# Block 2 of a two-block kernel: POOL's work taken over by DVE, and the units of v put ahead of the convolved ones

## The chip, the cores and the metric

One core of a Trainium2 chip runs the kernel; the other cores do nothing. The metric is device microseconds of one execution, as the median of several. Three runs of the kernel before took 1039.68, 1042.36 and 1042.78 us. The engines are named as in the profile: PE multiplies matrices, DVE and POOL work on vectors, ACT evaluates functions and copies, SP issues the transfers.

## The reference

Two blocks work on 256 tokens of 1024 features in fp32. The first is a Mamba-like mixer followed by a mixture of 32 experts; the change doesn't touch it, except for its last additions to `h`. The second block, of which the change reorders the mixer's half, is

```python
h = rms_norm(x, norm1)
lru_x, lru_g, q, k, v, g, z = jnp.split(h @ w_in, SPLIT_IDX, axis=-1)
lru_x = causal_depthwise_conv_2(lru_x, conv_w, conv_b)
lru_o = rg_lru(lru_x, lru_wa, lru_ba, lru_wi, lru_bi, lru_lambda) * jax.nn.gelu(lru_g)
log_alpha = jax.nn.log_sigmoid(z @ gla_w_alpha + gla_b_alpha) / GATE_TAU
o = gla_chunk_causal(q * q_scale, k, v, log_alpha)
gla_o = rms_norm(o, gla_norm) * jax.nn.silu(g)
x = x + jnp.concatenate([lru_o, gla_o], axis=-1) @ w_out
```

`rg_lru` takes two sigmoids of small block-diagonal products of the convolved `lru_x`, and runs a linear recurrence over the tokens. `gla_chunk_causal` is a gated linear attention in four chunks of 64 tokens, whose decays come from `z`. A gated feed-forward network follows.

## The kernel before, in words

Every large product is done in three passes: a weight tile is split into a rounded part `hi` (ACT, L329) and the rest `lo` (L330), and PE adds hi by hi, hi by lo and lo by hi. One column tile of 128 outputs with 1024 inputs is a **unit**: a split, 24 products of 128x256 (L339 to L341), and an `after` that takes the result out of PSUM. A unit of v (`v_unit`) is two of the eight rows of inputs by all 512 columns, in 12 products of 128x512 (L1672 to L1674).

`run_units` writes the order out by hand, since the engines run their instructions in program order and wait by semaphores. In turn i it emits the work registered with `at_pre(i)`, the split of unit i+2, unit i's products, the `after` of unit i-1, and then the work registered with `at(i)`. There are four buffers each of `hi` and `lo`, so that the split of unit i+4 waits for unit i's products.

The units of block 2's mixer before are: 0 z; 1, 2 k; 3, 4 q; 5 to 8 lx (the convolved ones); 9 to 12 v; 13 to 16 lg; 17 to 20 g; 21 to 28 the output projection. The split of units 1 and 2 is done ahead, at block 1's end. The tuple `P2` names the units whose `lo` POOL computes instead of DVE: 4 to 12.

The row scales (the norm's reciprocal roots) come late, and unscaled products wait for them in PSUM. `sums2` takes the sums of squares on ACT, `scales2` (L1451 to L1455 and `rsqrt_of`) the roots on DVE, `across` (L286) writes them on a diagonal `dg`, and PE spreads them over the partitions (`rsp`, L290) ahead of unit `SCALE`, which is 5. From then on the waiting results of z, k and q are scaled into SBUF, and all later ones directly. z's own small product with `wal` (`zf`, L1604) follows one turn later; `zexp`, ten polynomial steps in pieces of `STEPS`, and `la` make the decays of it; two exponentials and `kq_decay` apply them to k and q.

A unit of lx is scaled into `rg` (L1516), weighted by ACT (L1519), convolved by three DVE steps (L1524, "rest"), multiplied with the block-diagonal weights `wab` by PE (`gate_mm`, L1537, two turns later and ahead of that turn's unit), passed through two sigmoids by ACT (L1542) and multiplied by POOL (`ix`, L1543). `lru_exp`, `lru_q` and `lru_u` prepare the recurrence. `k_turn`, `scores` and `update` are the attention's small products from turn 13 on; `attend` (L1741, L1744) uses the last state `st` ahead of unit 17.

Of the kernel before, what the change touches and what calls it, by code (L numbers as in the profile page):

```python
# [8 lines left out]
F32 = mybir.dt.float32  # L9
# [17 lines left out]
WARM3 = 10  # L27
WARM4 = 5
K1 = (0, 1)
SH1 = 1  # L30
STEPS = (4, 3)
GAINS = 15
P2 = (4, 5, 6, 7, 8, 9, 10, 11, 12)
KT = 13
LEAD = 5
WARM2 = 4
# [33 lines left out]
def kernel(ctx: ExitStack, tc: tile.TileContext, *aps, dbg=None, stage=9):  # L70
# [276 lines left out]
    def at(i, f, *args):  # L347
        due.setdefault(i, []).append((f, args))

    def later(n, f, *args):  # L350
        at(cur[0] + n, f, *args)
# [112 lines left out]
    wo2, wfi, wfo = A["w_out_2"][0], A["w_ffn_in_2"][0], A["w_ffn_out_2"][0]  # L464
    skip = [1, 1, 0, 0]
    R2 = {}
    loads2 = deque([("kq", 1024), ("lx", 0), ("v", 1536), ("lg", 512), ("g", 2048), (("wo", 0), 0), (("wo", 1), 0)])
    for c in range(11):
        loads2.append((("fi", c), 0))
        if c % 2 == 1:  # L470
# [3 lines left out]
    def load_next2():  # L474
        if loads2:
            nm, c0 = loads2.popleft()
            if nm[0] == "wo":
                R2[nm] = raw_rows(wo2, 4 * nm[1])
            elif nm[0] == "fo":
                R2[nm] = raw_rows(wfo, 4 * nm[1], min(4, NF - 4 * nm[1]))  # L480
            elif nm[0] == "fi":
                t = R2[nm] = raw_tile([128, 8, 2, 256])
                for i in range(2):
                    c0 = i * 128 * NF + nm[1] * 256
                    nc.sync.dma_start(t[:, :, i, :], wfi[:, c0:c0 + 256].rearrange("(k p) c -> p k c", p=128))
            elif nm == "kq":
                t = R2[nm] = raw_tile([128, 8, 512])
                for c in (256, 0):
                    nc.sync.dma_start(t[:, :, c:c + 256], wcols("w_in_2", c0 + c, 256))
            else:  # L490
                R2[nm] = raw_cols("w_in_2", c0)
# [98 lines left out]
    def col_unit(src, c0, after, m=128, tag="mm", lo_last=False):  # L590


        def sp():
            return hilo(src()[:, :, c0:c0 + m], (8, m))

        def mm(w):
            o = ps.tile([128, T], F32, name="mm", tag=tag, bufs={"mm": 3, "op": 2, "pp": 2}.get(tag, 1))
            if lo_last:
                for k in range(8):
                    P.matmul(o[:m], w[0][:, k, :], hnh[:, k, :], start=(k == 0), stop=False)  # L600
                    P.matmul(o[:m], w[0][:, k, :], hnl[:, k, :], start=False, stop=False)
                for k in range(8):
                    P.matmul(o[:m], w[1][:, k, :], hnh[:, k, :], start=False, stop=(k == 7))
                return o
            for k in range(8):
                mm3(o[:m], w[0][:, k, :], w[1][:, k, :], hnh[:, k, :], hnl[:, k, :], k == 0, k == 7)
            return o

        return sp, mm, after
# [279 lines left out]
    gains = []  # L889
# [237 lines left out]
    with ExitStack() as pp:  # L1127
# [240 lines left out]
        def last_rows(g):  # L1368
            for (a, n, ns), tag in zip(HALF, (("p2", 1), ("py0", 1), ("py1", 1), ("gp", 1))):
                combine(g, a, n, tag)  # L1370
                if not a:
                    G.tensor_tensor(X2["g"][:, a, ns], h[:, a, ns], gains[1][:, ns], op=ALU.mult)  # L1372
                if (a, n) == K1:
                    split2(1)
            sums2(h, "sh", 0)
            if not SH1:
                sums2(h, "sh", 1)

        def sums2(src, acc, a):
            for n in range(2):  # L1380
                S.activation(X2["x"], src[:, a, n * 512:(n + 1) * 512], AF.Square, accum_out=X2[acc][:, a, n:n + 1])
# [58 lines left out]
    with ExitStack() as pc:  # L1440
# [22 lines left out]
            dump("x2", h)  # L1463
            more_bufs()

        def gains2():
            for n in range(2):
                ns = slice(n * 512, (n + 1) * 512)
                V.tensor_tensor(X2["g"][:, 1, ns], h[:, 1, ns], gains[1][:, ns], op=ALU.mult)

        psm = ExitStack()
        ps = psm.enter_context(tc.tile_pool(name="psC", bufs=1, space=PSUM, reuse_waits="tile"))
# [1 line left out]
        def buf(name, tag=None, dt=F32):  # L1474
            return mw.tile([128, 4, T], dt, name=name, tag=tag or name)

        SCALE = 5


        wab = [mw.tile([128, 4, 128], F32, name=f"wab{i}", tag=f"wab{i}") for i in range(2)]  # L1480
# [59 lines left out]
        def gate_act(t, p):  # L1540
            for i, (dst, c) in enumerate(((rg, c_ba), (ix, c_bi))):
                S.activation(dst[:, t, :], p[:, i, :], AF.Sigmoid, bias=cols2[:, c + t:c + t + 1])  # L1542
            G.tensor_tensor(ix[:, t, :], ix[:, t, :], xf[:, t, :], op=ALU.mult)  # L1543


        def lru_exp(t):
            S.activation(al[:, t, :], rg[:, t, :], AF.Exp, scale=sp8[:, 4 + t:5 + t])
            S.activation(rg[:, t, :], rg[:, t, :], AF.Tanh, scale=sp8[:, t:t + 1])
            if t == 3:
                G.tensor_tensor(s2, al, al, op=ALU.mult)  # L1550

        def lru_q():
            V.scalar_tensor_tensor(s2, s2, 1.0, rg, op0=ALU.add, op1=ALU.mult)
# [53 lines left out]
        def zexp():  # L1607
            for j in range(2):
                V.tensor_scalar(zb[:, j, :], Z["p"][:, j, :], cols2[:, c_gb + j:c_gb + j + 1], None, op0=ALU.add)
            S.activation(zu, zb, AF.Abs)  # L1610
            S.activation(zu, zu, AF.Exp, scale=-1.0)
            S.activation(small.tile([128, 1], F32, name="one"), ones[:, 0:1], AF.Sigmoid)
            poly = log1p_steps(zu, za)
            def steps(n):
                for _ in range(n):
                    poly.pop(0)()
                if poly:
                    later(1, steps, STEPS[1])
                else:
                    later(1, la)  # L1620

            later(1, steps, STEPS[0])

        def la():
            V.scalar_tensor_tensor(zb, zb, 0.0, za, op0=ALU.min, op1=ALU.subtract)
            for j in range(2):
                V.tensor_tensor_scan(zu[:, j, :], cmask, zb[:, j, :], 0.0, op0=ALU.mult, op1=ALU.add)
            bv = zu.rearrange(c4, c=4)
            be = bv[:, :, :, 63:64]
            V.tensor_tensor(za.rearrange(c4, c=4), be.to_broadcast([128, 2, 4, 64]), bv, op=ALU.subtract)  # L1630
            later(2, lambda: [S.activation(za, za, AF.Exp, scale=1.0 / 16),
                              S.activation(eb.unsqueeze(3), be, AF.Exp, scale=1.0 / 16)])
            later(2, kq_decay)

        def kq_decay():
# [5 lines left out]
            return lambda o: V.tensor_tensor(kd[:, j, :], o, rsb, op=ALU.mult)  # L1641

        def after_q(j):
            def f(o):
                V.scalar_tensor_tensor(qs[:, j, :], o, 0.125, rsb, op0=ALU.mult, op1=ALU.mult)
                if j == 1:
                    load_next2()

            return f

        def k_turn():
            p = ps.tile([128, 2, 256], F32, name="tp", tag="tp")
# [51 lines left out]
        def scores(a):  # L1704
            sT[a] = mw.tile([128, 4, 128], F32, name="sT", tag=("zu", "za")[a])
            ts = slice(a * 128, (a + 1) * 128)
            for s in range(2):
                p = ps.tile([128, 2, 128], F32, name="sc", tag=("tq", "ss")[s])
                r = slice(s * 64, s * 64 + 64)
                for j in range(2):  # L1710
                    P.matmul(p[:, j, :], kd[r, j, ts], qs[r, j, ts], start=True, stop=True)
                later(0, lambda p=p, s=s: V.tensor_tensor(sT[a][:, s::2, :], p,
                                                          diag[:, None, :].to_broadcast([128, 2, 128]), op=ALU.mult))
# [122 lines left out]
        def src2(nm):  # L1836
            return lambda: R2[nm]

        def from_scale(f):
            return lambda o: at(SCALE, f, o)  # L1840

        units = [narrow_unit(lambda: wz2, from_scale(after_z), tag="ss")]
        units += [col_unit(src2("kq"), 256 + j * 128, from_scale(after_k(j))) for j in range(2)]
        units += [col_unit(src2("kq"), j * 128, from_scale(after_q(j)), tag=("mm", "op")[j])
                  for j in range(2)]
        units += [col_unit(src2("lx"), t * 128, after_lx(t), tag="mm" if t else "op") for t in range(4)]
        units += [v_unit(i) for i in range(4)]
        units += [col_unit(src2("lg"), t * 128, after_lg(t)) for t in range(4)]
        units += [col_unit(src2("g"), t * 128, after_g(t)) for t in range(4)]
        units += [row_unit2(i) for i in range(8)]  # L1850
# [13 lines left out]
            at_pre(23 + i, gla_scale, i)  # L1864
            at(23 + i, gla_split, i)
        for t in range(4):
            at(14 + t // 2, lru_exp, t)
        at(16, lru_q)
        at(17, lru_u)
        for t in range(4):  # L1870
# [1 line left out]
            at(19 + t // 2, lru_out, t)  # L1872
            at(20 + t // 2, lru_lo, t)
        at(18, lru_gelu)
        at(0, gains2)
        if SH1:
            at(1, sums2, h, "sh", 1)
        for a in range(2):
            at(2, sums2, X2["g"], "sg", a)
        at(2, scales2)  # L1880
        at_pre(SCALE, lambda: across_mm(dg, rsb, ps.tile([128, T], F32, name="rsp", tag="tq")))
        at(3, rows2_)
        at(1, masks)
        at(6, chunks)
        at(GAINS, lambda: gains.extend([gain_rows("norm2_2", nc.gpsimd), gain_rows("final_norm_2", nc.gpsimd)]))
        early3 = []
        for j in range(2):
            at(len(units) - 2 + j, lambda j=j: early3.append(hilo(R2["fi", 0][:, :, j, 0:128], (8, 128))))
        run_units(units, ready=early2, pool=lambda i: i in P2)
        psm.close()  # L1890
        mix.close()
        dump("x3", h)
# [145 lines left out]
```

## Time and profile before

| | |
|---|---|
| median of 3 runs | 1042.36 us (1039.68 to 1042.78) |
| the profiled execution | 1042.26 us, of which the span of its instructions is 1040.5 us |
| busy over the span | PE 884.6, PEld 625.4, DVE 433.0, ACT 318.5, POOL 146.9 us |
| PE on the chain that ended last | 27%, DVE 4%, DMA 1% |
| mean granted clock of PE | 0.907 |

The span falls into block 1's mixer (about the first 190 us), the experts, in which the transfers are busy nearly throughout (to about 715 us), block 2's mixer (715 to 845 us), and its feed-forward network. In the last 180 us PE is at work almost without a break. The change is in block 2's mixer, between 720 and 800 us of the span, and that is the stretch to read: for each idle time of PE, which engine ended it, and what that engine did meanwhile.

### The profile page before, as it was taken

How to read it: one execution, taken by the hardware profiler on the slowest of the kernel's cores; microseconds unless marked ns; L12 is line 12 of the kernel's file. 1: busy time of each engine (PE TensorE's matmuls, PEld its weight loads, DVE VectorE, ACT ScalarE, POOL GpSimd, SP SyncE). 2: the span in 40 equal slices, each digit the busy share in tenths (PEclk: the TensorE clock that was granted, in tenths of full speed). 3: DMA queues.
4: the chain of work that ended last, by engine and by line, in shares of the span. 5: the costliest groups of instructions: out<-in, count | busy, mean ns of one | idle time of the engine just before them, and what ended most of it. 6: DMA issues, size and time to landing. Idle time of an engine off the chain costs nothing. (4 is left out here: it accounts for less than half of the span.)

```text
span 1040.5 us, 13656 instructions
## 1 busy us (share of the span) xinstructions
PE 884.6 (85%) x5675; PEld 625.4 (60%) x5676; DVE 433.0 (42%) x756; ACT 318.5 (31%) x533; POOL 146.9 (14%) x127
## 2 busy tenths in 40 slices
PE   8999998999868695776768596679679999999997
PEld 8988887677414141412314151137668789999996
DVE  6897565653002010101001010104896677555554
ACT  6664454524001100000000000004456545444444
POOL 4232024001000000000000000001452222111112
PEclk9999998999878798788779788769889999999999
DMA  9594433357999999999999999996534435474401
GB/s 288 135 388 166 162 105 139 124 200 272 425 428 421 429 426 429 425 425 425 425 426 429 427 428 425 422 393 221 214 104 143 141 130 192 166 242 147 138 1 41
DMA packets 77392, 287.85 MB, mean 277 GB/s; under 512 B 12499, under 2 KB 41358, under 8 KB 65678
## 3 DMA queue, kind: packets, MB, share of 16 engines
q1 hardware_dynamic: 76486, 285.03, 70.1%
q0 software_dynamic: 592, 1.60, 0.4%
q8 instruction: 46, 0.75, 0.3%
q10 hardware_dynamic: 248, 0.30, 0.1%
q14 instruction: 20, 0.16, 0.0%
HBM read 285.87 MB, written 1.05 MB: 276 GB/s over the span
## 5 line engine op out<-in xcount | busy, mean ns | idle before, releaser
L339 PE MATMUL mm<-hnh,hi 128*128 128x256 f32 x808 | 233.3, 289 | 1.6 <-ACT cx L702 0.9
L341 PE MATMUL mm<-hnh,lo 128*128 128x256 f32 x808 | 228.2, 282 | 0.9 <-DVE lo L330 0.9
L340 PE MATMUL mm<-hnl,hi 128*128 128x256 f32 x808 | 227.8, 282 | 0.0
L1185 PE MATMUL p<-raw,xse 128*32 128x512 f32 x1008 | 162.3, 690 | 58.6 <-DMA raw<-in_w_gate_dram 54.6
L330 DVE TENSOR_TENSOR lo<-raw,hi 128x1024 fp32r<-128x1024 f32 x137 | 168.8, 1236 | 80.5 <-ACT hi L329 80.4
L329 ACT ACTIVATE hi<-raw 128x1024 fp32r<-128x1024 f32 x152 | 159.0, 1057 | 100.4 <-PE mm L340 39.6
L339 PEld LDWEIGHTS mm<-hnh,hi 128*128 128x128 f32 x808 | 153.4, 190 | 11.0 <-issue 7.5
L341 PEld LDWEIGHTS mm<-hnh,lo 128*128 128x128 f32 x808 | 153.4, 190 | 1.5 <-DVE lo L330 1.3
L340 PEld LDWEIGHTS mm<-hnl,hi 128*128 128x128 f32 x808 | 153.6, 190 | 0.9
L1185 PEld LDWEIGHTS p<-raw,xse 128*32 128x32 f32 x1008 | 37.8, 124 | 170.6 <-issue 86.2
L1211 PE MATMUL py<-raw,hs 128*32 128x512 f32 x496 | 88.0, 727 | 34.3 <-DMA raw<-in_w_down_dram 29.1
L1250 DVE TENSOR_TENSOR h<-h,pc 128x512 f32<-128x512 f32 x32 | 20.5, 683 | 135.7 <-PE pc L1248 135.7
L1211 PEld LDWEIGHTS py<-raw,hs 128*32 128x32 f32 x496 | 19.3, 128 | 94.7 <-DMA raw<-in_w_down_dram 44.6
L1372 POOL TENSOR_TENSOR g<-h,gain 128x512 f32<-128x512 f32 x2 | 3.5, 1786 | 483.3 <-DVE h L1250 483.3
L1168 PE MATMUL gp<-oh,xnf 128*128 128x128 f32 x256 | 65.6, 430 | 4.8 <-ACT xse L1175 4.8
L1168 PEld LDWEIGHTS gp<-oh,xnf 128*128 128x128 f32 x256 | 62.1, 334 | 6.8 <-ACT xse L1175 6.8
L1239 DVE SCALAR_TENSOR_TENSOR lo<-py,gs,hi 128x512 fp32r<-128x512 f32 x14 | 10.5, 751 | 112.9 <-ACT hi L1238 112.1
L1923 POOL TENSOR_TENSOR sgf<-sgf,rsb 128x256 f32<-128x256 f32 x22 | 31.7, 1440 | 134.4 <-ACT sgf L1922 134.4
L1192 ACT ACTIVATE sg<-p 128x512 f32<-128x512 f32 x8 | 4.8, 598 | 143.8 <-PE p L1185 133.5
L330 POOL TENSOR_TENSOR lo<-raw,hi 128x1024 fp32r<-128x1024 f32 x15 | 37.2, 2493 | 39.9 <-ACT hi L329 39.9
L1238 ACT ACTIVATE hi<-py,gs 128x512 fp32r<-128x512 f32 (+1 forms) x15 | 10.1, 673 | 103.9 <-PE py L1211 103.7
L1202 ACT ACTIVATE hs<-p 128x512 f32<-128x512 f32 x8 | 4.8, 597 | 111.2 <-PE p L1200 111.2
(472 smaller groups left out, 1155.0 us busy)
## 6 DMA issues: line engine op xcount, KB each, us to landing
raw<-in_w_gate_dram SPq DMA_DIRECT2D x32, 2048.0 KB
raw<-in_w_up_dram SPq DMA_DIRECT2D x31, 2048.0 KB
raw<-in_w_down_dram SPq DMA_DIRECT2D x28, 2048.0 KB
raw<-in_w_in_dram SPq DMA_DIRECT2D x14, 2048.0 KB
raw<-in_w_ffn_in_dram SPq DMA_DIRECT2D x22, 1024.0 KB
raw<-in_w_out_dram SPq DMA_DIRECT2D x6, 2048.0 KB
raw<-in_w_ffn_out_dram SPq DMA_DIRECT2D x5, 2048.0 KB
raw<-in_w_down_dram SPq DMA_DIRECT2D x12, 512.0 KB
```

The lines of the kernel that those rows point to most:

```text
L329: S.activation(hv[:, r], src[:, r], AF.Copy)
L330: lo_on[0].tensor_tensor(lv, src, hv.bitcast(F32), op=ALU.subtract)
L339: P.matmul(o, wh, xh, start=first, stop=False)
L340: P.matmul(o, wh, xl, start=False, stop=False)
L341: P.matmul(o, wl, xh, start=False, stop=last)
L1168: P.matmul(p[:, kk, :], xn[:, a, 4 * hf + kk::8], OT[g][:, a, :], start=(a == 0), stop=(a == 1))
L1185: P.matmul(p[r], XS[g][:, k, r], ew(4 * g + i, m, k), start=(k == 0), stop=(k == 7))
L1211: P.matmul(PY[g][n][r], HT4[g][:, f, r], ew(4 * g + i, "d", f)[:, n * 512:(n + 1) * 512], start=(f == 0), stop=(f == 3))
L1238: S.activation(yh, y, AF.Copy, scale=gs)
L1239: V.scalar_tensor_tensor(yl, y, gs, yh.bitcast(F32), op0=ALU.mult, op1=ALU.subtract)
L1250: V.tensor_tensor(h[:, a, ns], h[:, a, ns], p, op=ALU.add)
L1923: G.tensor_tensor(t, t, rsb, op=ALU.mult)
```

## The change

It takes POOL's vector work out of block 2's first units, and reorders them.

- POOL's two products of h with the gain (L1372), its nine `lo` (units 4 to 12), its four `ix` and the square of `al` go to DVE. The two sums of squares of g's second half go from ACT to DVE (`sums_g1`), as products with an accumulator.
- The units of v come before those of lx: 5 to 8 are v now, and 9 to 12 lx. The loads of v and lx change places.
- `SCALE` goes from 5 to 6, `STEPS` from pieces of 4 and 3 to pieces of 5. The fills of `diag` and `cmask` (`chunks`) go from turn 6 to turn 1, those of `wab` (`masks`) from 1 to 2, `scales2` from 2 to 3, `rows2_` from 3 to 4, `lru_exp` one turn back, the two decay exponentials one turn ahead, followed by the load of the sigmoid's table. Some PSUM tags change, so that q's second result waits in `tp`, which `zf` uses.

```diff
-STEPS = (4, 3)
+STEPS = (5, 5)
-P2 = (4, 5, 6, 7, 8, 9, 10, 11, 12)
@@ last_rows
                 combine(g, a, n, tag)
-                if not a:
-                    G.tensor_tensor(X2["g"][:, a, ns], h[:, a, ns], gains[1][:, ns], op=ALU.mult)
+                V.tensor_tensor(X2["g"][:, a, ns], h[:, a, ns], gains[1][:, ns], op=ALU.mult)
@@ gains2 becomes sums_g1
-        def gains2():
+        def sums_g1():
             for n in range(2):
-                ns = slice(n * 512, (n + 1) * 512)
-                V.tensor_tensor(X2["g"][:, 1, ns], h[:, 1, ns], gains[1][:, ns], op=ALU.mult)
+                x = X2["g"][:, 1, n * 512:(n + 1) * 512]
+                V.scalar_tensor_tensor(xf.rearrange("p a t -> p (a t)")[:, :512], x, 1.0, x, op0=ALU.mult, op1=ALU.mult,
+                                       accum_out=X2["sg"][:, 1, n:n + 1])
-        SCALE = 5
+        SCALE = 6
@@ gate_act, lru_exp
-            G.tensor_tensor(ix[:, t, :], ix[:, t, :], xf[:, t, :], op=ALU.mult)
+            V.tensor_tensor(ix[:, t, :], ix[:, t, :], xf[:, t, :], op=ALU.mult)
-                G.tensor_tensor(s2, al, al, op=ALU.mult)
+                V.tensor_tensor(s2, al, al, op=ALU.mult)
@@ zexp, la
-            S.activation(small.tile([128, 1], F32, name="one"), ones[:, 0:1], AF.Sigmoid)
-            later(2, lambda: [S.activation(za, za, AF.Exp, scale=1.0 / 16),
-                              S.activation(eb.unsqueeze(3), be, AF.Exp, scale=1.0 / 16)])
+            later(1, lambda: [S.activation(za, za, AF.Exp, scale=1.0 / 16),
+                              S.activation(eb.unsqueeze(3), be, AF.Exp, scale=1.0 / 16),
+                              S.activation(small.tile([128, 1], F32, name="one"), ones[:, 0:1], AF.Sigmoid)])
@@ units and turns
-        units += [col_unit(src2("kq"), j * 128, from_scale(after_q(j)), tag=("mm", "op")[j])
+        units += [col_unit(src2("kq"), j * 128, from_scale(after_q(j)), tag=("mm", "tp")[j])
                   for j in range(2)]
-        units += [col_unit(src2("lx"), t * 128, after_lx(t), tag="mm" if t else "op") for t in range(4)]
         units += [v_unit(i) for i in range(4)]
+        units += [col_unit(src2("lx"), t * 128, after_lx(t)) for t in range(4)]
-            at(14 + t // 2, lru_exp, t)
+            at(15 + t // 2, lru_exp, t)
-        at(0, gains2)
-        if SH1:
-            at(1, sums2, h, "sh", 1)
-        for a in range(2):
-            at(2, sums2, X2["g"], "sg", a)
-        at(2, scales2)
+        at(0, sums2, h, "sh", 1)
+        at(0, sums_g1)
+        at(1, sums2, X2["g"], "sg", 0)
+        at(3, scales2)
+        at(4, load_next2)
-        at(3, rows2_)
-        at(1, masks)
-        at(6, chunks)
+        at(4, rows2_)
+        at(1, chunks)
+        at(2, masks)
-        run_units(units, ready=early2, pool=lambda i: i in P2)
+        run_units(units, ready=early2)
```

Three places show what moves. The first is DVE at the start of block 2's units. `h<-h,pc` are block 1's last additions, `g` is h by the gain, `sg` a sum of squares, `lo` the rest of a split, `w` the first of the scales. Before:

```order
L1250 TENSOR_TENSOR h<-h,pc 128x512 x2
L1469 TENSOR_TENSOR g_4475<-h,gain 128x512 x2
L330 TENSOR_TENSOR lo<-raw,hi 128x1024
L1486 MEMSET wab_4680 128x512
L1489 COPY wab_4680<-wa_144 64x4x64 x2
L1486 MEMSET wab_4681 128x512
L1489 COPY wab_4681<-wi_145 64x4x64 x2
L1451 TENSOR_TENSOR w_4673<-sh 128x2
```

And of the changed kernel, from the same additions on:

```order
L1248 TENSOR_TENSOR h<-h,pc 128x512
L1369 TENSOR_TENSOR g_4475<-h,gain 128x512
L1464 SCALAR_TENSOR_TENSOR xf,sg<-g_4475 128x512 x2
L328 TENSOR_TENSOR lo<-raw,hi 128x1024
L1488 MEMSET diag 128x128
L1490 MEMSET diag 64x64 x2
L1491 MEMSET cmask 128x256
L1492 MEMSET cmask 128x4
L328 TENSOR_TENSOR lo<-raw,hi 128x1024
L1482 MEMSET wab_4682 128x512
L1485 COPY wab_4682<-wa_144 64x4x64 x2
```

Each split now has its `lo` on DVE, and the fills stand between them. After these rows come the rest of the `wab` fills, one more `lo` and the scales.

The second place is ACT from the spread scales `rsb` on. `hi` is the rounded part of a split, `zu` the two functions of z's gate, `vt` v's result, `xf` the weighting of lx. Before:

```order
L386 ACTIVATE rsb<-rsp 128x256
L329 ACTIVATE hi<-raw 128x1024
L1519 ACTIVATE xf<-rg,cols_141 128x256
L1610 ACTIVATE zu<-zb 128x512
L1611 ACT_TABLE_LOAD
L1611 ACTIVATE zu<-zu 128x512
L1612 ACT_TABLE_LOAD
L1612 ACTIVATE one<-ones 128x1
L329 ACTIVATE hi<-raw 128x1024
L1519 ACTIVATE xf<-rg,cols_141 128x256
L329 ACTIVATE hi<-raw 128x1024
```

And of the changed kernel:

```order
L384 ACTIVATE rsb<-rsp 128x256
L327 ACTIVATE hi<-raw 128x1024
L1606 ACTIVATE zu<-zb 128x512
L1607 ACT_TABLE_LOAD
L1607 ACTIVATE zu<-zu 128x512
L327 ACTIVATE hi<-raw 128x1024 x2
L1669 ACTIVATE vt<-op,w_4676 128x512 x2
L327 ACTIVATE hi<-raw 128x1024
L1515 ACTIVATE xf<-rg,cols_141 128x256
L327 ACTIVATE hi<-raw 128x1024
L1515 ACTIVATE xf<-rg,cols_141 128x256
```

The first weighting of lx, which stood ahead of the functions of z's gate, stands behind four splits and v's result now.

The third place is DVE in the units of lg. `sT` are masked scores, `st` the attention's states, `gl` a scaled lg, `s` the recurrence's input. Before:

```order
L1712 TENSOR_TENSOR sT<-sc,diag 128x2x128 x2
L1696 COPY st_4695<-tp 128x256
L330 TENSOR_TENSOR lo<-raw,hi 128x1024
L1569 TENSOR_TENSOR gl<-mm,rsb 128x256
L1699 SCALAR_TENSOR_TENSOR st_4696<-st_4695,eb,tp 128x128 x2
L330 TENSOR_TENSOR lo<-raw,hi 128x1024
L1569 TENSOR_TENSOR gl<-mm,rsb 128x256
L1553 SCALAR_TENSOR_TENSOR s_4844<-s_4844,rg 128x1024
L1699 SCALAR_TENSOR_TENSOR st_4697<-st_4696,eb,tp 128x128 x2
```

And of the changed kernel:

```order
L1703 TENSOR_TENSOR sT<-sc,diag 128x2x128 x2
L1687 COPY st_4697<-tp 128x256
L328 TENSOR_TENSOR lo<-raw,hi 128x1024
L1565 TENSOR_TENSOR gl<-mm,rsb 128x256
L1539 TENSOR_TENSOR ix<-ix,xf 128x256
L1690 SCALAR_TENSOR_TENSOR st_4698<-st_4697,eb,tp 128x128 x2
L328 TENSOR_TENSOR lo<-raw,hi 128x1024
L1565 TENSOR_TENSOR gl<-mm,rsb 128x256
L1546 TENSOR_TENSOR s_4880<-al 128x1024
L1549 SCALAR_TENSOR_TENSOR s_4880<-s_4880,rg 128x1024
L1690 SCALAR_TENSOR_TENSOR st_4699<-st_4698,eb,tp 128x128 x2
```

`ix` and the square of `al` stand between the steps of the states; in the two turns ahead of these rows an `ix` and three steps of the convolution stand between a `gl` and the scores in the same way.

## Rows read from the trace of the kernel before

**Rows 1.** Busy time by stretch: PE, PEld, DVE, ACT, POOL, then clock and DMA.
```profile
721.50:735.50 14.00, 13.53 (x112) 12.96 (x112) 13.26 (x15) 11.78 (x23) 8.33 (x4) 1.00 1.04 377
735.50:743.60 8.10, 0.06 (x1) 0.06 (x1) 7.59 (x20) 0.00 (x0) 4.87 (x3) 0.80 0.45 184
...
765.40:771.20 5.80, 5.80 (x14) 4.61 (x15) 5.59 (x10) 2.27 (x4) 2.19 (x2) 0.50 0.00 0
...
783.20:800.40 17.20, 17.20 (x150) 15.80 (x148) 11.24 (x20) 10.21 (x15) 5.91 (x5) 1.00 0.54 184
```

**Rows 2.** PE's waits from 715 to 800 us: total, times, longest.
```profile
PE rsp L290 <- DVE dg L286: 8.0, 1, 8.0
PE tp L1537 <- DVE xf L1524: 6.0, 1, 6.0
```

**Rows 3.** POOL's timeline: start, duration, instruction, count, idle time before and releaser.
```profile
733.31 7.05 POOL L330 TENSOR_TENSOR lo<-raw,hi 128x1024 fp32r<-128x1024 f32 x3 [1.29 <-ACT hi L329]
```

**Rows 4.** DVE's timeline up to the scales.
```profile
721.93 1.22 DVE L330 TENSOR_TENSOR lo<-raw,hi 128x1024 fp32r<-128x1024 f32 x1 [0.46 <-ACT hi L329]
723.08 1.28 DVE L1250 TENSOR_TENSOR h<-h,pc 128x512 f32<-128x512 f32 x2
...
735.91 2.18 DVE L1451 TENSOR_TENSOR w<-sh 128x2 f32<-128x2 f32 x1
...
738.12 2.27 DVE L1453 TENSOR_SCALAR w<-w 128x2 f32<-128x2 f32 x1
...
743.01 0.48 DVE L286 TENSOR_SCALAR dg<-ident,w 128x128 f32<-128x128 f32 x2
```

**Rows 5.** Line 1489 alone, durations min/median/max in ns.
```profile
L1489 DVE COPY wab<-wi x2: 286/1355/2424, 733.2 to 733.5; 64x256 f32<-64x256 f32 x2
```

**Rows 6.** DVE's timeline behind the scales.
```profile
743.40 1.41 DVE L1462 TENSOR_SCALAR h<-g,w 128x1024 f32<-128x1024 f32 x2
...
746.44 0.74 DVE L1641 TENSOR_TENSOR kd<-mm,rsb 128x256 f32<-128x256 f32 x2
...
753.23 1.51 DVE L1524 SCALAR_TENSOR_TENSOR xf<-rg,cols,xf 128x255 f32<-128x255 f32 x3
...
755.12 4.24 DVE L400 SCALAR_TENSOR_TENSOR za<-za,zu 128x512 f32<-128x512 f32 x3
...
765.11 2.13 DVE L400 SCALAR_TENSOR_TENSOR za<-za,zu 128x512 f32<-128x512 f32 x3
...
775.98 1.27 DVE L1627 TENSOR_TENSOR_SCAN zu<-cmask,zb 128x256 f32<-128x256 f32 x2
...
794.56 1.21 DVE L1553 SCALAR_TENSOR_TENSOR s<-s,rg 128x1024 f32<-128x1024 f32 x1
```

**Rows 7.** ACT's timeline.
```profile
751.69 1.28 ACT L1611 ACT_TABLE_LOAD   x1
752.98 0.63 ACT L1611 ACTIVATE zu<-zu 128x512 f32<-128x512 f32 x1
...
767.61 0.60 ACT L1519 ACTIVATE xf<-rg,cols 128x256 f32<-128x256 f32 x1 [5.61 <-DVE rg L1516]
...
768.82 1.05 ACT L329 ACTIVATE hi<-raw 128x1024 fp32r<-128x1024 f32 x1
...
783.76 0.50 ACT L1547 ACTIVATE al<-rg,sp 128x256 f32<-128x256 f32 x1
```

**Rows 8.** PE's timeline.
```profile
748.70 1.12 PE L1604 MATMUL tp<-zs,wal 16*128 16x256 f32 x4
...
771.77 1.03 PE L1537 MATMUL tp<-xf,wab 128*128 128x256 f32 x4
772.44 0.58 PE L1672 MATMUL op<-hi,hnh 128*128 128x512 f32 x1
...
798.17 0.88 PE L1744 MATMUL op<-qd,st 64*128 64x64 f32 x6
800.42 0.39 PE L339 MATMUL mm<-hnh,hi 128*128 128x256 f32 x1
```

More of the change, by code (lines that the diff above doesn't have):

```diff
@@ L29 @@
 K1 = (0, 1)
-SH1 = 1
-STEPS = (4, 3)
+STEPS = (5, 5)
 GAINS = 15
-P2 = (4, 5, 6, 7, 8, 9, 10, 11, 12)
 KT = 13
@@ L466 @@
     R2 = {}
-    loads2 = deque([("kq", 1024), ("lx", 0), ("v", 1536), ("lg", 512), ("g", 2048), (("wo", 0), 0), (("wo", 1), 0)])
+    loads2 = deque([("kq", 1024), ("v", 1536), ("lx", 0), ("lg", 512), ("g", 2048), (("wo", 0), 0), (("wo", 1), 0)])
     for c in range(11):
@@ L1375, in last_rows @@
             sums2(h, "sh", 0)
-            if not SH1:
-                sums2(h, "sh", 1)
         def sums2(src, acc, a):
@@ L1643, in after_q @@
         def after_q(j):
[L1644 to L1649, printed above, removed]
+            return lambda o: V.scalar_tensor_tensor(qs[:, j, :], o, 0.125, rsb, op0=ALU.mult, op1=ALU.mult)
         def k_turn():
@@ L1707, in scores @@
             for s in range(2):
-                p = ps.tile([128, 2, 128], F32, name="sc", tag=("tq", "ss")[s])
+                p = ps.tile([128, 2, 128], F32, name="sc", tag=("op", "ss")[s], bufs=2 - s)
                 r = slice(s * 64, s * 64 + 64)
```

## The prediction

> **What bounds the kernel now.** The page gives PE 85% of the span, and the stretch of the change is one of the few in which it waits for another engine. I read PE's waits there first: only two are long, 8.0 us for the scales on DVE and 6.0 us for a convolution on DVE [rows 2]. While they last DVE is busy nearly all the time (7.59 of 8.10 us), and POOL works beside it for 4.87 us [rows 1]. After the second wait PE runs 5.80 us at the lower of its two levels (granted 0.50, that is 1.2 GHz) [rows 1]; in the first stretch the mean fell to 0.80. From 783.2 to 800.4 PE is busy for all 17.20 us with only 11.24 us of DVE work beside it [rows 1]. So DVE bounds the front, PE the rear.
>
> DVE's timeline says why the front is slow. Three splits on POOL from 733.31, 2.35 us each, end at about 735.7, 738.0 and 740.4 [rows 3]. A copy that takes 0.29 us alone takes 2.42 and ends at 735.9 [rows 5]; two operations on two numbers per partition take 2.18 and 2.27 us and end at 738.1 and 740.4 [rows 4]. About once per POOL instruction a DVE instruction stands until POOL's is over. The same shows in the polynomial, 4.24 us for three steps that take 2.13 elsewhere [rows 6]. With POOL idle I price these at their short durations.
>
> **The change part by part.** Prices: a `lo` 1.15 us (start to start, rows of 721.93 and 723.08), a 128x512 addition 0.61 (two in 1.28, overlapping) [rows 4]. One of the sixteen small operations of the scales costs 0.2: thirteen lie between 740.4 and 743.0 [rows 4]. A unit on PE costs 2.9, from 112 products in 13.53 us [rows 1]. The squares with accumulator aren't shown. From below they are one polynomial step, 0.71 [rows 6], from above twice that; I take 0.76, and both ends move the sum by -0.1 and +1.3.
>
> *From the first `lo` to the scales.* DVE starts at 721.9 as before. Up to `dg` it now does five `lo` (5.8), eight additions and products (4.9), two squares (1.5), the fills of `diag` and `cmask` (five, each at most like the short copy, 1.0), those of `wab` (four short copies, and two fills taken as 0.5, 2.2) and the scales (3.7). Two waits of 0.5 and 0.3 come in, since ACT's sums now stand ahead of unit 3's split. Together 19.8: `dg` at 741.7, against 743.5 [rows 4]. PE waits 2.7 us ahead of unit 3, 1.0 ahead of `rsp` and 0.6 ahead of v's second unit in place of 8.0, and has v's first unit done by then. It leads by 1.8+2.9 = 4.7 us.
>
> *From the scales to the first small product of lx.* DVE does a `lo`, the scaling of h (1.41), two `lo`, z, k and q (seven at about 0.37) [rows 6]: 7.5 us, to 749.2. `zf` stands ahead of v's third unit on PE and takes the PSUM tile in which q's second result waits. So PE, done at 745.6, waits 3.7 us. `zf` takes 1.1 [rows 8]; DVE's two additions of the bias end at 751.4. ACT then takes two functions of 0.63 and a table load of 1.28, and only behind them unit 10's `hi` (1.0) [rows 7]. DVE has nothing between that bias and unit 10's `lo`: it stands for 3.8 us, to 755.2. Then follow that `lo` and two more (3.5), ten polynomial steps (6.9), a scaling (0.36), the scans with what lies around them (2.6), a `lo` and a scaling (1.5) and the convolution (1.47) [rows 6]: 16.3, to 771.5. PE, with five units behind `zf`, is done at 764.9 and waits 6.7 us for it. This is the old wait of 6.0 us again.
>
> *To the first unit of lg.* In turn 12 ACT has a weighting (0.5), the decay's exponentials (0.85), the sigmoid's load with its first use (1.5) and a split (1.0) before DVE's next `lo`: DVE stands for 2.5. Then `ix`, on DVE now, waits for a weighting and two sigmoids, 1.2 us on ACT [rows 7], 1.4 with the handovers, 1.5 in all. k and q are decayed at 778.7, the next convolution ends at 780.2, and lg's first unit starts at 781.0. Before it started at 783.2 [rows 1]. PE's half clock after the wait costs nothing here, since it would wait for k anyway. So 2.2 us of lead are left.
>
> *The units of lg.* Before, lx's small products lay between units of v, `ix` was POOL's, and PE never waited here. Now DVE's work in turns 13 to 16 is 4.7 (`lo`, scaling, `ix`, convolution, copy, masks), 4.4, 2.4 and 4.4 (with the square of `al` and `lru_q`, 1.15 each by the form of 1.21 in [rows 6]): 15.9 us, about what PE has there. Three times `ix` waits for the sigmoids (1.5, 1.5, 0.9). In turn 16 the `lo` waits for a split behind a table load and four functions of 0.5 [rows 7], 3.4 us; the square waits 0.5 more. That is 780.2+15.9+7.8 = 803.9 for the last state, which `attend` needs ahead of unit 17. Before, that product started at 798.17 and unit 17 at 800.42 [rows 8]. It starts 5.7 us later. Behind it the order is the old one and PE the bound, so nothing takes the delay up or adds to it.
>
> The table load is priced at 1.28 us by its row: the next function starts 0.01 us behind it, at 752.98 [rows 7]. The Trainium skill (ScalarE: Activation LUTs, section What ACT_TABLE_LOAD costs) adds a drain of about 1.4 us to each switch. By that the loads on this path would bring 5.7 to 9.9; the trace shows no such gap, and the row decides.
>
> The loads keep their places in the queue, v's in lx's. The buffer of k and q is free after unit 4's split, and the output projection's tile is needed only in turn 19, so I cost the transfers at nothing; a late v would be seen as PE waiting ahead of unit 5.
>
> The sum is 5.7 us on the profiled execution: its span 1040.5 becomes 1046.2, its 1042.26 becomes 1048.0. That execution lies 0.1 below the median of the runs, so 1048.0 stands for the median.
>
> **The rivals.** *The clock falls in the shorter waits too.* Before it fell in waits of 8.0 and 6.0 us. Mine of 3.7 (ahead of `zf`) and 3.5 (ahead of the last states) lie below these, and no row shows one of that size in this stretch. If it falls in both, `zf` takes 1.0 longer with all behind it, and the work from 804 on runs 5.8 us at half speed as in [rows 1], which loses 2.9: 1051.9. The Trainium skill (TensorE: Matmul & The Clock Gate, section What's actually happening) has the clock follow recent activity, which speaks for it; the rows at 8.0 and 6.0 agree as far as they go.
>
> *DVE's waits for ACT are half what I count* in turns 13 to 16, because the sigmoids or functions come earlier than handed on here. Then 3.9 of the 7.8 us go, and the time is 1044.1, no change. For it speaks that ACT is idle for long there; against it that each wait is a chain in program order.
>
> *Faster.* The place is unit 10's `lo` behind the two functions of z's gate. If DVE doesn't stand there and in turn 12 (3.8+2.5+1.5), nor for the sigmoids, lx's first product comes at 767.7, and DVE's remaining 4.7+15.9 us bring the last state to 788.3; PE's own work from there (four small products of lx at 0.67 [rows 8], five units, some 4 us of the attention's) is 21 us and brings it to 788.9. That is 9.3 before 798.17: 1033. It decides from the point at which more than 5.7 of the 15.6 us of DVE's waits are gone; with 9 gone the time is 1039. For it speaks that POOL's stalls do go. Against it: the new waits come from the order of ACT's program, which no shorter DVE instruction changes.
>
> **How the numbers follow.** The forecast of 1048.0 has 0.51 (its own range 1045.5 to 1051, from handovers of 0.02 to 0.1 us and the squares), the clock 0.17, no change 0.18, faster 0.14. About 0.3%, 3 us, is what a measurement of this kernel can tell from no change: 1039.2 to 1045.5. Slower is 0.51+0.17 = 0.68, the same 0.18, faster 0.14. The range from 1041 to 1053 leaves out the faster case and the tail of the clock's.
>
> **What would show it.** Right: no DVE instruction of the scales or the polynomial above 1 us; `dg` near 742; PE waiting some 3 to 4 us for `zf` and 6 to 7 for the first product of lx; DVE standing nearly 4 us ahead of unit 10's `lo` with ACT's `hi` as releaser; waits of PE in the units of lg, the largest ahead of `attend`, and unit 17 near 806. Wrong: unit 17 before 800, PE without waits from lg on, or long DVE instructions that stay although POOL is idle.

## The result, and the profile after

| | before | after |
|---|---|---|
| median of 7 runs | 1039.68 us | 1049.79 us (1044.20 to 1051.47) |
| the profiled execution, its span | 1042.26, 1040.5 us | 1050.22, 1048.4 us |
| mean granted clock | 0.907 | 0.901 |

The ratio over all runs is 1.0082, with an interval of 1.0057 to 1.0106: 8.5 us slower (5.9 to 11.0); the two medians lie 10.1 us apart. 1048.0 was forecast. In this trace the first `lo` of block 2 starts at 722.78, 0.85 us later than at 721.93 [rows 4]. That lies ahead of the vector work that was changed, and in the traces of the experiments below it starts anywhere from 718.0 to 722.9, so I measure the stretch from that `lo` on.

PE's waits after, from 715 to 815 us (total, times, longest; the line numbers are two to nine lower than before's):

```profile
PE tp L1533 <- DVE xf L1520: 5.8, 2, 4.9
PE tp L1600 <- DVE qs L1640: 3.3, 1, 3.3
PE op L1735 <- DVE st L1690: 2.2, 1, 2.2
PE mm L339 <- DVE lo L328: 1.5, 2, 0.9
PE sc L1702 <- DVE sT L1703: 1.3, 1, 1.3
...
PE tp L1682 <- DVE st L1687: 1.0, 1, 1.0
```

The 8.0 us for `dg` and the 6.0 for a convolution [rows 2] are gone. In their place stand 3.3 us for `zf`, 4.9 for lx's first product, and three shorter waits for the scores and states, where there were none. DVE's timeline after, at the places of [rows 4, 6] (start, duration, instruction, idle time before and releaser):

```profile
722.78 1.23 DVE L328 TENSOR_TENSOR lo<-raw,hi 128x1024 fp32r<-128x1024 f32 x1 [0.46 <-ACT hi L327]
...
730.35 0.68 DVE L1464 SCALAR_TENSOR_TENSOR xf<-g 128x512 f32<-128x512 f32 x1
730.96 0.08 DVE L1464 DVE_READ_ACCUMULATOR xf<-g 128x1 f32 x1
...
738.65 0.15 DVE L1446 TENSOR_TENSOR w<-sh 128x2 f32<-128x2 f32 x1
...
738.84 0.17 DVE L1448 TENSOR_SCALAR w<-w 128x2 f32<-128x2 f32 x1
...
741.63 0.48 DVE L284 TENSOR_SCALAR dg<-ident,w 128x128 f32<-128x128 f32 x2
...
755.17 1.23 DVE L328 TENSOR_TENSOR lo<-raw,hi 128x1024 fp32r<-128x1024 f32 x1 [3.59 <-ACT hi L327]
...
773.60 1.23 DVE L328 TENSOR_TENSOR lo<-raw,hi 128x1024 fp32r<-128x1024 f32 x1 [2.31 <-ACT hi L327]
...
776.55 0.43 DVE L1539 TENSOR_TENSOR ix<-ix,xf 128x256 f32<-128x256 f32 x1 [1.39 <-ACT ix L1538]
...
782.49 0.43 DVE L1539 TENSOR_TENSOR ix<-ix,xf 128x256 f32<-128x256 f32 x1 [1.40 <-ACT ix L1538]
...
788.97 0.42 DVE L1539 TENSOR_TENSOR ix<-ix,xf 128x256 f32<-128x256 f32 x1 [1.90 <-ACT ix L1538]
...
794.56 0.42 DVE L1539 TENSOR_TENSOR ix<-ix,xf 128x256 f32<-128x256 f32 x1 [1.26 <-ACT ix L1538]
...
798.81 1.23 DVE L328 TENSOR_TENSOR lo<-raw,hi 128x1024 fp32r<-128x1024 f32 x1 [3.31 <-ACT hi L327]
```

Operations of the scales that took 2.18 and 2.27 us beside POOL [rows 4] take 0.15 and 0.17 with POOL idle. From 755 on DVE stands seven times for ACT, 15.2 us in all. PE's timeline after, for [rows 8]:

```profile
749.54 1.13 PE L1600 MATMUL tp<-zs,wal 16*128 16x256 f32 x4 [3.33 <-DVE qs L1640]
...
771.44 2.04 PE L1533 MATMUL tp<-xf,wab 128*128 128x256 f32 x4 [4.95 <-DVE xf L1520]
...
780.52 0.47 PE L337 MATMUL mm<-hnh,hi 128*128 128x256 f32 x1
...
803.16 0.69 PE L1735 MATMUL op<-qd,st 64*128 64x64 f32 x2 [2.20 <-DVE st L1690]
...
806.39 0.58 PE L337 MATMUL mm<-hnh,hi 128*128 128x256 f32 x1
```

lg's first unit starts at 780.52, earlier than before (783.2); unit 17 at 806.39 in place of 800.42. `attend`'s products with the last state are the last two of six. They start at 803.16; before, where [rows 8] show the first of the six at 798.17, they started at 798.66. Busy time by stretch (PE, PEld, DVE, ACT, POOL, clock, DMA):

```profile
777.20:803.20 26.00, 20.17 (x161) 17.97 (x161) 17.80 (x34) 13.66 (x23) 0.00 (x0) 0.99 0.26 82
803.20:806.40 3.20, 3.20 (x13) 2.74 (x13) 2.02 (x4) 1.07 (x2) 2.34 (x1) 0.50 0.00 0
806.40:810.80 4.40, 4.40 (x27) 4.40 (x27) 1.71 (x2) 3.67 (x4) 0.55 (x2) 0.66 0.19 20
```

Where PE had been busy for all of lg's units [rows 1], it is busy for 20.17 of 26.00 us; then its clock falls to 0.50, the lower of its two levels, and is at 0.66 in the mean until 810.8. Counted from the first `lo`, the products with the last state come 3.65 us later than before (4.50 by the times of the traces, less 0.85), unit 17 5.1 (78.49 before, 83.61 after), and the end of the span 7.05 (318.57 before, 325.62 after).

### The profile page after: what moved, and what is told of

Its sections match the earlier page's. It is cut to its first block, busy times and chain, and to the rows that moved or that the text cites. A ratio compares the mean times of both kernels' runs of the same rounds, so it can differ in the third digit from the quotient of the medians.

```text
span 1048.4 us, 13639 instructions
## 1 busy us (share of the span) xinstructions
PE 889.9 (85%) x5675; PEld 631.4 (60%) x5676; DVE 431.2 (41%) x776; ACT 317.2 (30%) x529; POOL 117.0 (11%) x111
## 5 line engine op out<-in xcount | busy, mean ns | idle before, releaser
L328 DVE TENSOR_TENSOR lo<-raw,hi 128x1024 fp32r<-128x1024 f32 x146 | 179.1, 1230 | 90.3 <-ACT hi L327 90.1
L1236 ACT ACTIVATE hi<-py,gs 128x512 fp32r<-128x512 f32 (+1 forms) x15 | 10.1, 673 | 104.4 <-PE py L1209 104.3
L309 PE MATMUL po<-hi,al 128*128 128x512 f32 x88 | 34.9, 397 | 0.0
```

The lines of the kernel that those rows point to most:

```text
L309: P.matmul(po[a, j], yl[:, ts], wh[:, 0, ns], start=False, stop=end)
L328: lo_on[0].tensor_tensor(lv, src, hv.bitcast(F32), op=ALU.subtract)
```

## The experiments

Each is compared by its ratio to runs of the kernel before on the same chip. "Stretch" is the time from z's first product to unit 17's: 78.9 us before, 84.0 after.

**e1: `ix` back on POOL.** The changed kernel with

```
-            V.tensor_tensor(ix[:, t, :], ix[:, t, :], xf[:, t, :], op=ALU.mult)
+            G.tensor_tensor(ix[:, t, :], ix[:, t, :], xf[:, t, :], op=ALU.mult)
```

> The changed kernel with one thing undone: the four products ix go back to POOL. Theory (the delay in the units of lg comes from DVE standing in program order for ACT's sigmoids): DVE's four waits ahead of ix, 1.4+1.4+1.9+1.3 = 6.0 us in the changed kernel's trace, go, PE's waits ahead of the scores and the second state shrink, and the kernel is 2 to 4 us faster than the changed one (about 1046). DVE's wait of 3.3 us for a split behind the exponentials stays. Rival (DVE's sum of work bounds these units): four products of 0.4 us go, 1.5 us at most, no measurable change. Rival (lock): POOL's ix at 0.7 to 1.2 us each holds DVE up again, no gain.

Measured: 1042.04 us, ratio 1.0019 (1.0001 to 1.0036), 0.6% below the changed kernel's; stretch 79.3. That is more than expected. The waits for the scores and states are gone; those for `zf`, for lx's first product and for the last state stay (PE's waits):

```profile
PE tp L1533 <- DVE xf L1520: 5.2, 2, 4.9
PE tp L1600 <- DVE qs L1640: 3.3, 1, 3.3
PE op L1735 <- DVE st L1690: 2.2, 1, 2.2
```

So the four `ix`, 0.43 us each, cost some 6 us by the sigmoids that DVE waits for ahead of them. The last state stays late: DVE, no longer held up earlier, now stands in one piece for a split behind the recurrence's functions on ACT (its timeline):

```profile
791.48 1.23 DVE L328 TENSOR_TENSOR lo<-raw,hi 128x1024 fp32r<-128x1024 f32 x1 [5.60 <-ACT hi L327]
```

**e2: lx ahead of v again.** The changed kernel with the units, their loads and `SCALE` in the order of before (the edit of the units alone is shown).

```
-        units += [v_unit(i) for i in range(4)]
-        units += [col_unit(src2("lx"), t * 128, after_lx(t)) for t in range(4)]
+        units += [col_unit(src2("lx"), t * 128, after_lx(t), tag="mm" if t else "op") for t in range(4)]
+        units += [v_unit(i) for i in range(4)]
```

> The changed kernel with the units of lx ahead of v again (and SCALE 5, which that order needs); all work that left POOL stays off it. Theory (the order of the units costs, taking work off POOL gains): PE's waits ahead of the scores, the states and attend (5 us together in the changed kernel) go, since v's units lie between the small products of lx again; PE still waits some us in the units of lx, where DVE has per unit a lo, a scaling, a convolution and the polynomial (5 us against PE's 3.5). 4 to 9 us faster than the changed kernel, 1036 to 1042 if the kernel before takes 1040 beside it. Rival (the lo on DVE are what costs): within 2 us of the changed kernel.

Measured: 1046.93 us, ratio 1.0063 (1.0042 to 1.0084); stretch 83.8. The order gives back some 0.2%, less than the two intervals can tell from nothing. My theory that it was the main cost falls: with lx first the waits for the scores and states are gone, but PE waits longer for lx's products (9.5 us in three waits, where the changed kernel has 5.8 in two).

**e3: only the nine `lo` to DVE.** The kernel before with `P2 = ()`.

> The kernel before with one part of the change alone: the nine lo of units 4 to 12 on DVE in place of POOL; POOL keeps its products with the gain and ix. Theory: DVE gets 9 x 1.15 = 10.4 us of work and loses some 17 us of standing beside POOL; dg comes about 5 us earlier and PE's wait of 8.0 us ahead of rsp falls to 1 to 3; in the units of lx DVE bounds and PE waits 4 to 8 us in pieces. 2 to 6 us faster than the kernel before. Rival (DVE becomes the bound): 2 us or more slower than the kernel before.

Measured: 1036.12 us, ratio 0.9952 (0.9937 to 0.9967), faster than before; stretch 75.4. DVE's rows of the scales:

```profile
730.69 0.15 DVE L1451 TENSOR_TENSOR w<-sh 128x2 f32<-128x2 f32 x1
...
730.88 0.17 DVE L1453 TENSOR_SCALAR w<-w 128x2 f32<-128x2 f32 x1
...
733.67 0.48 DVE L286 TENSOR_SCALAR dg<-ident,w 128x128 f32<-128x128 f32 x2
...
749.84 1.23 DVE L330 TENSOR_TENSOR lo<-raw,hi 128x1024 fp32r<-128x1024 f32 x1 [5.09 <-ACT hi L329]
```

DVE has more to do and its `dg` comes 14.4 us after its first `lo` (719.26), where it took 21.1 before. So this part of the change is a gain. In the trace before no engine waits for a `lo` of POOL in this stretch, so I read the gain as DVE's time and not as an earlier `lo`. The wait behind the functions of z's gate, 5.09 us here, is in both orders.

**e4: only the order of the units.** The kernel before with v ahead of lx, the loads and q's tag `tp`; POOL keeps its `lo`.

> The kernel before with the other part alone: v's units ahead of those of lx (loads and q's PSUM tag with them), POOL keeps its work. Theory (the order costs by itself, since lx's small products now fall among the units of lg): PE keeps the 8.0 us ahead of rsp, waits for zf behind q's tile (2 to 4 us), for the first product of lx (5 us or more) and again in the units of lg: 4 to 10 us slower than the kernel before. Rival (the order is harmless, only the work on DVE costs): within 2 us of the kernel before.

Measured: 1055.83 us, ratio 1.0146 (1.0121 to 1.0172); stretch 91.9. That is 15 us, more than the 4 to 10 expected. PE's waits:

```profile
PE rsp L290 <- DVE dg L286: 8.3, 1, 8.3
PE tp L1537 <- ACT hi L329: 7.9, 1, 7.9
PE tp L1537 <- DVE sT L1712: 5.7, 2, 4.6
PE op L1744 <- DVE st L1699: 2.8, 1, 2.8
```

And DVE's timeline at the scales and at the polynomial:

```profile
732.93 2.18 DVE L1451 TENSOR_TENSOR w<-sh 128x2 f32<-128x2 f32 x1
...
735.14 2.27 DVE L1453 TENSOR_SCALAR w<-w 128x2 f32<-128x2 f32 x1
...
750.66 10.65 DVE L400 SCALAR_TENSOR_TENSOR za<-za,zu 128x512 f32<-128x512 f32 x6
```

By itself the order costs 15 us; beside DVE's `lo` 1 to 2 (e2, and e10 against e8). The parts don't add. As I read the rows, the scales are as late as before, so PE stands for `dg` first, and then for convolutions that only begin behind the whole of z's gate. In that gate POOL holds DVE up again: four of its `lo` run from 752.71 to 763.57, and the nine polynomial steps beside them take 14.91 us (the row shows the first six), where nine of 0.71 [rows 6] would take 6.4. These 8.5 us lie in DVE's unbroken work up to lx's first convolution, for which PE stands 7.9 us, and by these rows they are more than half of the 15.

**e5: e2 with `ix` on POOL.** The two edits of e1 and e2 together.

> The second experiment's kernel (all of the change, but lx ahead of v) with ix on POOL. There DVE stood 2.8 and 1.4 us for the sigmoids ahead of ix, inside the chain of the convolutions for which PE waited 9.5 us in three pieces. Theory (ix on DVE puts ACT's sigmoids into DVE's program order, whatever the units' order): these two waits go and two products of 0.4 with them, PE's waits for the convolution fall to 4 to 6 us, 4 to 6 us faster than that kernel. Rival (not ix, but the heavier polynomial pieces and the splits fill DVE): at most 1.5 us faster.

Measured: 1040.18 us, ratio 1.0009 (0.9995 to 1.0023); stretch 79.7. `ix` costs 5.6 us in this order as well. What is left between e3 and e5, 5.9 us, is the rest of the change, most of it at the front: products, squares and fills on DVE ahead of the scales, the scales a turn later, `STEPS`, the exponentials, the PSUM tags, and behind them the square of `al` and the later `lru_exp`.

**e6: the table of Exp loaded early.** The changed kernel with

```
+        at(SCALE, lambda: S.activation(small.tile([128, 1], F32, name="exp1"), ones[:, 0:1], AF.Exp))
```

> The changed kernel with one more ACT instruction: an exponential of one column right behind rsb, which loads the table of exponentials while ACT is idle, 5 us before z's gate needs it. Theory (unit 10's lo stands behind z's functions on ACT, and all of DVE behind it): DVE's wait ahead of that lo falls from 3.6 to 2.3 us, and PE's wait for the first product of lx from 4.9 to about 3.7; 1 to 2 us faster than the changed kernel, somewhat more if PE's clock then doesn't fall. Rival (that wait lies beside others and is given back): no change.

Measured: 1049.05 us, ratio 1.0095 (1.0078 to 1.0112): nothing gained. DVE's wait ahead of unit 10's `lo` fell from 3.59 to 2.30 us, and PE's longest, for lx's first product, from 4.9 to 3.7 (its waits, the first row). But that product came only 0.3 us sooner behind the first `lo` (48.3 us in place of 48.7), since `zf` ahead of it ran at half clock, 2.07 us in place of 1.13 (PE's timeline, the second row). And the clock was lower in lg's units, where the changed kernel's was 0.99, and in unit 17, 0.50 for 5.50 us in place of 0.66 for 4.40 (windows):

```profile
PE tp L1533 <- DVE xf L1520: 4.5, 2, 3.7
...
747.22 2.07 PE L1600 MATMUL tp<-zs,wal 16*128 16x256 f32 x4 [3.42 <-DVE qs L1640]
```

```profile
784.90:791.30 6.40, 6.40 (x32) 5.89 (x32) 3.29 (x8) 1.78 (x3) 0.00 (x0) 0.59 1.00 318
...
804.70:810.20 5.50, 5.50 (x27) 5.50 (x27) 1.71 (x2) 3.67 (x4) 1.60 (x2) 0.50 0.32 71
```

So in this trace the clock gave back what DVE gained. One profile can't say whether it did so in every run.

**e7: e3 with the tables moved.** Exp's load early as in e6, and the sigmoid's a turn later.

> The third experiment's kernel (the kernel before with the lo on DVE, 0.5% faster than it) with the table of exponentials loaded ahead in the same way, and the sigmoid's one turn later. There DVE stood 5.1 us ahead of a lo behind two functions and two loads (2 x 1.28 us), and PE 4.2 us for the first product of lx behind that. Theory: the two loads leave that chain, DVE's wait falls to 2.5 us and PE's to 1.6 us, its clock stays up behind it; 2 to 4 us faster than that kernel, about 1033 where the kernel before takes 1040. Rival (the sigmoid's load then holds the next turn up as long): no change.

Measured: 1033.57 us, ratio 0.9942 (0.9927 to 0.9956); stretch 72.5. DVE's wait of 5.09 us became 2.31, PE's stretch is 2.9 us shorter, but the time differs from e3's by less than the intervals tell.

**e8: e5 with a shorter front.** The scales back at turn 2, and the fills of `wab` behind the Exp of z's gate, where DVE waits.

```
             S.activation(zu, zu, AF.Exp, scale=-1.0)
+            masks()
...
-        at(3, scales2)
+        at(2, scales2)
...
-        at(2, masks)
```

> The changed kernel with lx ahead of v, ix on POOL (as in e5), the scales back at turn 2, and the fills of wab emitted behind the Exp of z's gate, where DVE waits for ACT. Theory (what stands ahead of the scales in DVE's order sets the front): dg comes 3.4 us earlier than in e5 by a lo of 1.15 and fills of 2.2, rsp 16.4 us after the first product of z in place of 19.8, and the fills lie in DVE's wait of 3.6 us ahead of the next lo; the stretch from z to unit 17 is 77 us in place of 79.7, the time 2 to 3 us below e5's, ratio to before 0.998 to 0.999. Rival (behind the scales DVE is the bound anyway, so an earlier dg only moves the wait to the first product of lx): rsp is earlier, the wait for lx longer by as much, the stretch and the time within 1 us of e5's, ratio 1.001.

Measured: 1037.39 us, ratio 0.9979 (0.9965 to 0.9994), 0.3% (3 us) below e5's; stretch 76.4. As the theory had it: about half of the 5.9 us was the place of the scales and fills in DVE's order. The other half was not taken apart.

**e9: e7 with DVE's chain cut further.** The scaling of h on ACT, the fills of `diag` and `cmask` on POOL at turn 4, those of `wab` as in e8, and `rows2_` two turns later (the scaling alone is shown).

```
-                V.tensor_scalar(h[:, a, :], X2["g"][:, a, :], y1[:, a:a + 1], None, op0=ALU.mult)
+                S.activation(h[:, a, :], X2["g"][:, a, :], AF.Copy, scale=y1[:, a:a + 1])
```

> The kernel before with all lo on DVE, the Exp table loaded early and the load of the sigmoid's later (as in e7), and DVE's chain cut further: the scaling of h on ACT (two of 1.05 us while ACT is idle), the fills of diag and cmask on POOL at turn 4, those of wab behind the Exp of z's gate, where DVE waits. Theory (DVE's chain from z to the first product of lx is the bound): DVE has 1.4, 1.0 and 2.2 us less on that chain, PE's waits for zf and in lx's units (1.5, 1.5 and 1.7 in e7) shrink by 2 to 4 us, stretch from z to unit 17 about 69.5 us, ratio to before 0.990 to 0.992. Rival (the time is already PE's, at its lower clock, or ACT's): waits shrink but the stretch stays within 1 us of e7's 72.5, ratio 0.994.

Measured: 1029.46 us, ratio 0.9903 (0.9882 to 0.9924), the fastest of all: 10 us below before, and by the ratios 19 below the changed kernel; stretch 69.2. PE's waits:

```profile
PE tp L1537 <- DVE xf L1524: 5.3, 3, 2.1
...
PE tp L1604 <- DVE zs L1598: 0.7, 1, 0.7
...
PE rsp L290 <- DVE dg L286: 0.2, 1, 0.2
```

**e10: the changed kernel mended.** Its order of units, with `ix` on POOL (e1) and the two edits of e8.

> The changed kernel with its order of units (v ahead of lx) and three edits: ix back on POOL (as in e1), the scales at turn 2, the fills of wab behind the Exp of z's gate. Theory (the costs add: ix 0.5 to 0.6 per cent, the fills and scales 0.3 per cent, the order of the units 0.1 to 0.2): e8 and this one differ only in the order, so this comes out at a ratio to before of 0.999 to 1.000, 1038.5 to 1040 us. Rival (with v first PE reaches lx early and waits for its first product for whatever DVE has left to do, so that an earlier scale is lost there): as e1, ratio 1.002, with a wait for the first lx product above 5 us.

Measured: 1038.57 us, ratio 0.9991 (0.9980 to 1.0003); stretch 76.2. The time is the theory's, though the wait for lx's first product is 6.5 us as the rival had it: what the front gains at `rsp` and `zf` is partly spent there.

**e11: e9 with `ix` on DVE.** The edit of e1 the other way round.

> e9 with the four ix on DVE. Theory (ix costs DVE its wait of about 1.4 us for the sigmoids each time, and DVE sets the time in lx's and lg's units): four times 1.4 to 1.5 us, 5 to 6 us as from e5 to e2, ratio to before 0.995 to 0.996. Rival (with DVE's chain shortened the waits fit beside PE's work): under 2 us, ratio 0.990 to 0.992.

Measured: 1032.07 us, ratio 0.9930 (0.9913 to 0.9947), 2.8 us above e9 by the ratios, with an error as large: between the two expectations. Only two of the four `ix` wait (DVE's timeline):

```profile
751.18 0.42 DVE L1543 TENSOR_TENSOR ix<-ix,xf 128x256 f32<-128x256 f32 x1 [1.39 <-ACT ix L1542]
...
757.95 0.43 DVE L1543 TENSOR_TENSOR ix<-ix,xf 128x256 f32<-128x256 f32 x1 [1.39 <-ACT ix L1542]
...
762.91 0.42 DVE L1543 TENSOR_TENSOR ix<-ix,xf 128x256 f32<-128x256 f32 x1
```

So the price of such a wait hangs on what stands ahead of it: two products waited 1.4 us each, and the other two found the sigmoids done.

In one chain, in us against before: the nine `lo` on DVE -5.0 (e3); the rest of the front +5.9 (e5); `ix` on DVE +5.6 (e2); the order +2.0 (the changed kernel). By the intervals these differences have errors of 1.6, 2.1, 2.6 and 3.4 us. So the first three stand, and the price of the order is not told from nothing; e5 to e1 and e8 to e10 show it as 1.0 and 1.2, each within its error of some 2.

## Why the prediction was right, and which term was not

Direction and mechanism were right; in these points, times of the trace after less 0.85:

- *From the first `lo` to the scales.* The end of `dg` was forecast at 741.7 and measured at 741.3. The two squares took 1.35 us with their accumulator (1.5), and the stalls of some 2.2 us each beside POOL went. PE's waits were 2.3 us in all (0.51, 0.83, 0.94) where 4.3 were forecast, and none of them for `rsp`.
- *To lx's first small product.* PE waited 3.3 us for `zf` (3.7), DVE 3.59 for unit 10's `hi` (3.8), PE 4.95 for the product (6.7). It came at 770.6 against 771.5. DVE's idle time behind ACT's functions lies on its path: in e6 1.3 us of it went, `zf` at half clock brought 0.9 back, and the product came 0.3 us sooner.
- *To lg's first unit.* DVE waited 2.31 and 1.39 us (2.5 and 1.5); lg began at 779.7 (781.0).
- *The units of lg.* `ix` waited 1.40, 1.90 and 1.26 us (1.5, 1.5, 0.9), the `lo` of turn 16 3.31 (3.4), the square not at all (0.5). Together that is 7.9 us where 7.8 were counted, so the rival that halves these waits falls. The products with the last state were 3.65 us late. 5.7 were forecast, but the sum set its 803.9 against 798.17, the first of the six products; against 798.66 it says 5.2. DVE was 0.4 to 1.6 us earlier than the sum at each of these points.
- That behind it "nothing takes the delay up or adds to it" is the step that failed. Between `attend` and unit 17 another 1.5 us was added, and 1.9 behind it, 3.4 in all. The clock of the windows accounts for most of it: 3.20 us at 0.50 lose 1.6, 4.40 at 0.66 lose 1.5. No run held the clock fixed, so this is read, not tested. It is the rear half of the rival on the clock, near its price of 2.9. The front half came too, but behind `zf`, which took 1.13 us, full speed, after a wait of 3.33: from 751.3 to about 754.8 v's products ran at half speed, and this cost the path nothing, since PE then waited 4.95 us for lx's first product anyway. With 3.65 + 3.4 = 7.05 us the delay is 1.35 longer than the sum. The remaining 0.85 of this profile lies ahead of the first `lo`, and no experiment here explains it.

That the number itself came so near is in part luck. 1048.0 is a sum of 5.7 us on an execution of 1042.26, near the median of the three runs then at hand; the median of seven is 1039.68, and from there the same sum gives 1045.4, where 1049.79 was measured.

The table load cost 1.28 us, as priced, with the next function 0.02 behind it and no gap ahead of it. The extra drain that the Trainium skill (ScalarE: Activation LUTs, section What ACT_TABLE_LOAD costs) adds doesn't show in the trace after, at the place on ACT that [rows 7] show before:

```profile
752.26 1.28 ACT L1607 ACT_TABLE_LOAD   x1
753.56 0.63 ACT L1607 ACTIVATE zu<-zu 128x512 f32<-128x512 f32 x1
```

The prediction gave the whole loss to the new waits, without saying which part of the change brings which. The runs divide it: the `lo` alone were a gain of 5 us, and what lost it again was for the most part what was put on DVE beside them. That was not seen because the sum set the change as one against before, and did not price its parts apart.

## What to carry to other kernels

Work moved from POOL to DVE can cost DVE less than it saves, where each POOL instruction held one of DVE's up. Count then what stands in DVE's program order ahead of the instruction that others wait for: a 0.4 us product that waits 1.4 us for another engine can cost the wait and not only the product. Put fills and other free work where the engine waits anyway, and price the parts of a change one by one, since here one part gained 5 us and two others lost 11.5. Where several small waits come to stand in a stretch that had none, add a price for the clock behind them; here it was read from one trace.

## What the runs showed of the hardware

PE's granted clock fell behind waits shorter than the 8.0 and 6.0 us of before, and not always at once. Behind the 3.33 us ahead of `zf` it stayed at the higher level for 1.8 us (1.00 from 749.5 to 751.3) and then fell (0.51 from 751.3 to 753.0, up again by 755.0). PE's timeline after shows a product of v ahead of the fall and one behind it:

```profile
750.93 0.40 PE L1664 MATMUL op<-lo,hnh 128*128 128x512 f32 x1
...
751.86 0.63 PE L1664 MATMUL op<-lo,hnh 128*128 128x512 f32 x1
```

In e6 nearly the same wait, 3.42 us, ended with the clock already down: `zf`'s four products took 2.07 us. Behind 2.20 us that followed waits of 0.82, 1.33 and 1.04 it was at 0.50 at once (from 803.2 on). So the length of the last wait alone doesn't tell when the clock falls.

Two operations on two numbers take 2.18 and 2.27 us beside POOL's `lo` (e4, and before) and 0.15 and 0.17 without it (e3), and in e4 nine polynomial steps take 14.91 us beside four of POOL's `lo`. That the stalls would go was expected from the rows; that moving the nine `lo` is worth 5 us by itself stood in e3's expectation (2 to 6 us), but not in the prediction.
